# Layer 1's products of a two-layer decoder: one 512-column product and one of 256 columns against three of 256 columns, with one accumulator and displaced weight parts

## The chip, the cores and the metric

The kernel runs on one core of a Trainium2 chip. The metric is the device time of one execution in microseconds (us); less is better. Engines are named as in the profile: PE is the matrix engine, PEld its weight loads, DVE the vector engine, ACT the scalar engine, POOL GpSimd, SP the engine that issues the weight transfers.

## The reference, cut to what matters

The model has 16 meta tokens and 256 tokens of input, 2048 features, two layers and a feed-forward width of 8192. Layer 0 uses forgetting attention; layer 1 uses stick-breaking attention on a shared K/V stream. The last step drops the meta tokens, so in layer 1 only the shared K/V needs all 272 tokens; queries, output projection and feed-forward need 256.

```
for layer in range(DEPTH):                      # DEPTH = 2
    a = rms_norm(h, norm_attn[layer])
    if layer < N_A_LAYERS:
        proj = a @ fox_w_in[i]                  # q, k, v, forget gate
        h = h + forgetting_attention(...) @ fox_w_o[i]
    else:
        k_s, v_s = jnp.split(rms_norm(h, kv_norm) @ w_kv, 2, axis=-1)
        h = h + stick_breaking_attention(a @ sb_w_q[i], k_s, v_s) @ sb_w_o[i]
    h = h + jnp.square(jax.nn.relu(rms_norm(h, norm_mlp[layer]) @ w_up[layer])) @ w_down[layer]
return rms_norm(h, final_norm)[:, N_META:]
```

All of it is in float32, and the answer has to be near float32.

## The kernel before, in words

**Parts.** Activations are kept transposed: 16 chunks of 128 features, tokens along the row. A float32 number is multiplied on PE in the format float32r, which keeps fewer bits, so each operand is written as a sum of two parts, `hi` (rounded) and `lo` (the rest). A product of weight and activation is then three products: hi·hi, hi·lo and lo·hi; lo·lo is dropped. `Split` (L118) holds both parts of the 16 activation chunks in one tile with rows of 640 floats (`XROW`, L28); `ROWS` (L27) gives where in the row hi and lo begin: floats 48 and 368 in layer 0's tiles (272 tokens), 0 and 304 in layer 1's (256 tokens). The K/V stream of layer 1 has 272 tokens and layer 0's form.

**A group.** `gemm_group` (L183) computes 512 output features: four accumulators of 128 x 512 floats in PSUM (`accs`, L191), one for each m = 0..3. The 16 chunks of the contraction come in four steps kb of four chunks kc. Each step loads two transfers of 512 KB from SP (L207); ACT rounds the weights to `whi` (L218), DVE writes `wlo` as the difference (L219). The tiles `whi` and `wlo` have rows of 576 floats. `whi` is written from float 0 of the row; `wlo` from float 0 in layer 0's groups and from float 16 (64 bytes) in layer 1's groups that run in pairs (L211). In the build the tiles of weights and activations all begin at multiples of 256 bytes, and so do their rows.

**Order.** In kb 0 and 3 a run is one m with four kc, in kb 1 and 2 two kc with four m (L226 to L231). The products are chained so that PE gets them as written (`gemm_matmul`, L175; the profile gives all of them line L177). Each product has its own weight load.

- Layer 0's products (and K/V of layer 1) come one by one with 272 columns: for each m and kc `whi`·hi, `whi`·lo, `wlo`·hi into the same columns of the accumulator (L244 to L250).
- Layer 1's groups (query projection, output projection, up and down, 40 groups) run in pairs: in each run first all `whi` products, each with 512 columns, which read hi and lo of the chunk in one go (`sp.both`, L130) and write them into the two halves of the accumulator; then all `wlo`·hi products with 256 columns into the first half (L236 to L243).
- One m of the last group, the argument `apart` (L493), is done product by product as in layer 0.

**After a group.** Each accumulator is drained by `evac`. With two halves the residual add (L255) has two DVE instructions, and the query and up projections call `total` (L259), where ACT copies the second half (L263) and DVE adds the first (L264) ahead of the work that follows.

Of the kernel before, what the change touches and what calls it, by code (L numbers as in the profile page):

```python
# [12 lines left out]
ALU = mybir.AluOpType  # L13
AX = mybir.AxisListType

P = 128
# [7 lines left out]
QSCALE = 1.0 / math.sqrt(P)  # L24
N_FF = 4

ROWS = {0: (48, 368), M: (0, 304)}  # L27
XROW = 640  # L28

G_A0, G_M0, G_KV, G_A1, G_M1, G_FIN = range(6)  # L30
# [3 lines left out]
def yoco_kernel(ctx: ExitStack, tc: tile.TileContext, hT_in, gains, b_f, w_f, w_qkv0, w_o0, w_up, w_dn,  # L34
# [83 lines left out]
    class Split:  # L118


        def __init__(self, label, t0):
            n = T - t0
            self.t0 = t0
            rows = xs.tile([P, NC * XROW + 64], F32R, tag="x", name=f"x_{label}")
            hi, lo = ROWS[t0]
            rows = rows[:, hi:hi + NC * XROW].rearrange("p (c t) -> p c t", c=NC)
            d = lo - hi
            self.hi, self.lo = rows[:, :, :n], rows[:, :, d:d + n]

            self.both = rows[:, :, :2 * d].rearrange("p c (i t) -> p c i t", i=2)[:, :, :, :n]  # L130

    def split_chunk(sp, gi, c):

        g = g_sb[:, gi, c:c + 1]
# [45 lines left out]
                                                                        mybir.DependencyReason.DATA))  # L180
        queued[:] = [ins]

    def gemm_group(wblk, sp, t0, evac, before={}, after={}, load_x=None, pairs=False, apart=()):  # L183

        uid[0] += 1
        u = uid[0]  # L190
        accs = [pacc.tile([P, 512], F32, tag="acc", name=f"acc_{u}_{m}") for m in range(4)]  # L191
        n = T - t0
        for kb in range(4):
            src_w = wblk[kb].rearrange("p (k c) -> p k c", k=4)
            if kb in before:
                before[kb]()
            piece = 1 if load_x is not None and kb < 2 else 2
            raws = [wraw.tile([P, 2, 512], F32, tag="raw", name=f"raw_{u}_{kb}_{hf}") for hf in range(2)]
            for k0 in range(0, 4, piece):
                if load_x is not None:  # L200
                    load_x(range(4 * kb + k0, 4 * kb + k0 + piece))
                if load_x is not None and kb == k0 == 0:

                    for c0 in (0, 256):
                        nc.scalar.dma_start(raws[0][:, 0, c0:c0 + 256], src_w[:, 0, c0:c0 + 256])
                else:
                    nc.sync.dma_start(raws[k0 // 2][:, k0 % 2:k0 % 2 + piece], src_w[:, k0:k0 + piece])  # L207
            parts = []
            for hf in range(2):
                whi, wlo = (wspl.tile([P, 2, 576], F32R, tag=f"w{x}", name=f"w{x}_{u}_{kb}_{hf}") for x in ("hi", "lo"))  # L210
                whi, wlo = whi[:, :, :512], wlo[:, :, 16:528] if pairs else wlo[:, :, :512]  # L211
                boxes = [(o, piece, 0, 512) for o in range(0, 2, piece)]
                if load_x is not None and kb == hf == 0:
                    boxes[:1] = [(0, 1, 0, 256), (0, 1, 256, 512)]
                for o, no, c0, c1 in boxes:
                    src = raws[hf][:, o:o + no, c0:c1]
                    hp, lp = whi[:, o:o + no, c0:c1], wlo[:, o:o + no, c0:c1]
                    on_act = nc.scalar.activation(hp, src, AF.Copy)  # L218
                    on_dve = nc.vector.tensor_tensor(out=lp, in0=src, in1=hp.bitcast(F32), op=ALU.subtract)  # L219
                parts.append((whi, wlo))  # L220
            if kb in after:
                with tc.issue_after(on_act.ins), tc.issue_after(on_dve.ins):
                    after[kb]()


            if load_x is not None and kb == 0:  # L226
                runs = [([kc], range(4)) for kc in range(4)]
            elif kb in (0, 3):
                runs = [(range(4), [m]) for m in range(4)]
            else:  # L230
                runs = [(range(2 * hf, 2 * hf + 2), range(4)) for hf in range(2)]  # L231
            pinned[0] = load_x is None
            for kcs, ms in runs:
                paired = [m for m in ms if pairs and m not in apart]
                single = [m for m in ms if m not in paired]
                for kc in kcs:  # L236
                    for m in paired:
                        gemm_matmul(accs[m], parts[kc // 2][0][:, kc % 2, m * P:(m + 1) * P], sp.both[:, 4 * kb + kc],
                                    start=kb == kc == 0, stop=False)
                for kc in kcs:  # L240
                    for m in paired:
                        gemm_matmul(accs[m][:, :n], parts[kc // 2][1][:, kc % 2, m * P:(m + 1) * P],
                                    sp.hi[:, 4 * kb + kc], start=False, stop=kb == kc == 3)  # L243
                for m in single:  # L244
                    for kc in kcs:
                        wh, wl = (w[:, kc % 2, m * P:(m + 1) * P] for w in parts[kc // 2])
                        hi, lo = sp.hi[:, 4 * kb + kc], sp.lo[:, 4 * kb + kc]
                        gemm_matmul(accs[m][:, :n], wh, hi, start=kb == kc == 0, stop=False)
                        gemm_matmul(accs[m][:, :n], wh, lo, start=False, stop=False)
                        gemm_matmul(accs[m][:, :n], wl, hi, start=False, stop=kb == kc == 3)  # L250
                if kb == 3:
                    for m in ms:
                        evac(m, [accs[m][:, :n]] + ([accs[m][:, n:]] if m in paired else []))

    def residual_add(c, acc, t0):  # L255
        for a in acc:
            nc.vector.tensor_tensor(out=hT[:, c, t0:], in0=a, in1=hT[:, c, t0:], op=ALU.add)  # L257

    def total(acc, to):  # L259

        if len(acc) == 1:
            return acc[0]
        nc.scalar.copy(to, acc[1])  # L263
        nc.vector.tensor_tensor(out=to, in0=acc[0], in1=to, op=ALU.add)  # L264
        return to


    norm = Norm("a0", 0)
# [96 lines left out]
    for g in range(4):  # L365
# [2 lines left out]
        vT = att.tile([P, 4, T], F32, tag="vT", bufs=1, name=f"vT0_{g}")  # L368

        def evac_q(m, acc, qT=qT):  # L370
            nc.vector.scalar_tensor_tensor(out=qT[:, m, :], in0=acc[0], scalar=-QSCALE, in1=box["rstd"],
                                           op0=ALU.mult, op1=ALU.mult)

        def evac_kv(m, acc, t):
            nc.vector.tensor_tensor(out=t[:, m, :], in0=acc[0], in1=box["rstd"], op=ALU.mult)

        if g == 0:

            gemm_group(w_qkv0[0], xa, 0, lambda m, acc, qT=qT: nc.scalar.copy(qT[:, m, :], acc[0]),
                       after={kb: (lambda kb=kb: first_norm(kb)) for kb in range(4)}, load_x=load_x)  # L380
            gate_products()
            box["rstd"] = norm.finish()
            for m in range(4):
                evac_q(m, [qT[:, m, :]])
            forget_gates(box["rstd"])
        else:
            gemm_group(w_qkv0[3 * g], xa, 0, evac_q)
# [88 lines left out]
    def out_proj(w, ao, t0, gi, label):  # L476
        norm = Norm(label, t0)
        xm = Split(label, t0)
        for g in range(4):
            def evac(m, acc, g=g):  # L480
                c = 4 * g + m
                residual_add(c, acc, t0)
                split_chunk(xm, gi, c)
                norm.add(c)
            gemm_group(w[g], ao, t0, evac, pairs=t0 == M)
        return xm, norm

    def mlp(layer, xm, norm, t0, last_evac):
# [5 lines left out]
        for f in range(N_FF):  # L494
            u = Split(f"u{layer}_{f}", t0)
            for g in range(4):
                def evac(m, acc, g=g):
                    c = 4 * g + m
                    r = tmp.tile([P, T], F32, tag="relu", name=f"relu_{layer}_{f}_{c}")
                    u2 = tmp.tile([P, T], F32, tag="u2", name=f"u2_{layer}_{f}_{c}")  # L500
                    nc.vector.scalar_tensor_tensor(out=r[:, t0:], in0=total(acc, r[:, t0:]), scalar=0.0, in1=box["r"][:, t0:],
                                                   op0=ALU.max, op1=ALU.mult)
                    nc.scalar.activation(u2[:, t0:], r[:, t0:], AF.Square)
                    nc.scalar.activation(u.hi[:, c], u2[:, t0:], AF.Copy)
                    nc.vector.tensor_tensor(out=u.lo[:, c], in0=u2[:, t0:], in1=u.hi[:, c].bitcast(F32),
                                            op=ALU.subtract)
                gemm_group(w_up[layer, f, g], xm, t0, evac, {2: get_rstd} if f == g == 0 else {},
                           pairs=t0 == M)
            for g in range(4):
                def evac(m, acc, g=g):  # L510
                    residual_add(4 * g + m, acc, t0)
                    if f == N_FF - 1:
                        last_evac(4 * g + m)
                gemm_group(w_dn[layer, f, g], u, t0, evac, pairs=t0 == M,
                           apart=(3,) if layer == 1 and f == N_FF - 1 and g == 3 else ())

    xm, norm_m = out_proj(w_o0, ao, 0, G_M0, "m0")

# [17 lines left out]
    for g in range(4):  # L536
        def evac_q1(m, acc, g=g):
            q = qT1[g][:, m, :S]
            nc.vector.scalar_tensor_tensor(out=q, in0=total(acc, q), scalar=QSCALE, in1=box["rstd"][:, M:],
                                           op0=ALU.mult, op1=ALU.mult)  # L540
        def split_c(kb, g=g):
            for c in ([4 * kb + g - 1] if g < 3 else [4 * kb + 2, 4 * kb + 3]):
                split_chunk(xc, G_KV, c)

        gemm_group(w_q1[g], xq, M, evac_q1, {2: get_rstd1} if g == 0 else {},
                   after={kb: (lambda kb=kb: split_c(kb)) for kb in range(4)} if g else {}, pairs=True)

    ao = Split("o1", M)
    for g in range(4):
# [189 lines left out]
```

## Time and profile before

| | |
|---|---|
| median of 3 runs | 2315.99 us (2315.36 to 2316.57) |
| profiled execution | 2316.17 us, its span 2314.5 us |
| PE busy | 2303.4 us (100%), 16486 products |
| PEld busy | 2183.1 us (94%), 16486 loads |
| DVE, ACT, POOL busy | 1350.1 us (58%), 1064.1 us (46%), 40.8 us (2%) |
| granted PE clock, mean | 0.998 |
| DMA | 412 MB, 178 GB/s |

How to read it: a product of float32 (not float32r) stands in two records, so records are more than products in the program; a few records may be missing. A product is pipelined: its record lasts longer than the time until the next one starts, so what a product costs is the distance between starts. In a timeline, neighbouring instructions of one kind are merged: start, length from the first start to the last end, kind, and count. The first product of layer 1's query projection starts at about 1200 us, its K/V and attention lie between about 1304 and 1521 us; the output projection begins among the last of that work and lasts until about 1597 us, up and down from there to 2302 us.

### The profile page before, as it was taken

What the parts mean: (1) busy time and instruction counts of PE and PEld (TensorE: products, weight loads), DVE (VectorE), ACT (ScalarE), POOL (GpSimd) and SP (SyncE); (2) the same over time, 40 slices, a digit from 0 to 9 for tenths busy, and PEclk for the clock granted to TensorE, in tenths of its full rate; (3) what the DMA queues carried; (4) which work ended last, traced back from release to release, by engine and by line L of the source; (5) the groups of instructions that cost most, each with busy time, mean ns of one, the idle gap of its engine ahead of it and who ended that gap; (6) DMA issues with size and microseconds to landing.
All of it is one profiled execution on the core that took longest, in us unless ns stands there. A gap on an engine that the chain in (4) does not pass through costs nothing.

```text
span 2314.5 us, 39954 instructions
## 1 busy us (share of the span) xinstructions
PE 2303.4 (100%) x16486; PEld 2183.1 (94%) x16486; DVE 1350.1 (58%) x1923; ACT 1064.1 (46%) x1477; POOL 40.8 (2%) x58
## 2 busy tenths in 40 slices
PE   9999999999999999999999999999999999999998
PEld 9999999999999999999998999988888888888887
DVE  7665555655454455445566555566665665665665
ACT  6434344543344344344445444455543543543553
POOL 1000000000000000000000000000000000000000
PEclk9999999999999999999999999999999999999999
DMA  6545445455555555555555444455556556556563
GB/s 233 169 155 170 166 163 170 168 187 174 181 170 186 179 175 181 173 184 175 182 178 200 157 146 146 146 169 196 193 188 199 185 190 200 185 191 199 183 200 128
DMA packets 116630, 412.00 MB, mean 178 GB/s; under 512 B 13264, under 2 KB 16736, under 8 KB 116448
## 3 DMA queue, kind: packets, MB, share of 16 engines
q1 hardware_dynamic: 114560, 406.29, 52.7%
q10 hardware_dynamic: 1888, 3.16, 0.4%
q8 instruction: 129, 2.11, 0.4%
q14 instruction: 53, 0.43, 0.1%
HBM read 407.29 MB, written 2.11 MB: 177 GB/s over the span
## 4 chain that ended last, share of the span: by engine, by line
PE 99%; DVE 0%; DMA 0%; ACT 0%; issue 0%; SPq 0%; DVEq 0%; ACTq 0%
PE acc L177 96%; PE ps L407 0%; PE pza L586 0%; PE pv L340 0%; PE po L469 0%; PE po L625 0%; PE pzb L587 0%; PE po L626 0%; PE po L470 0%; DMA g_sb<-gains 0%; PE po L627 0%; DVE ob L681 0%; PE pf L306 0%; PE pf L307 0%; PE pta L601 0%; PE pta L602 0%
## 5 line engine op out<-in xcount | busy, mean ns | idle before, releaser
L219 DVE TENSOR_TENSOR wlo<-raw,whi 128x1024 fp32r<-128x1024 f32 (+1 forms) x773 | 931.6, 1217 | 741.8 <-ACT whi L218 740.6
L218 ACT ACTIVATE whi<-raw 128x1024 fp32r<-128x1024 f32 (+1 forms) x773 | 799.1, 1050 | 948.0 <-PE acc L177 873.8
L177 PE MATMUL acc<-x_u,whi 128*128 128x272 f32 (+2 forms) x3088 | 647.9, 321 | 0.0
L177 PE MATMUL acc<-x_m,whi 128*128 128x272 f32 (+1 forms) x3072 | 646.2, 322 | 0.0
L177 PEld LDWEIGHTS acc<-x_u,whi 128*128 128x128 f32 x3088 | 499.5, 188 | 26.6
L177 PEld LDWEIGHTS acc<-x_m,whi 128*128 128x128 f32 x3072 | 497.5, 188 | 27.2
L177 PE MATMUL acc<-x_u,wlo 128*128 128x272 f32 (+1 forms) x2048 | 443.3, 281 | 0.0
L177 PE MATMUL acc<-x_m,wlo 128*128 128x272 f32 (+1 forms) x2048 | 441.0, 281 | 0.0
L177 PE MATMUL acc<-x_a,whi 128*128 128x272 f32 (+1 forms) x1792 | 360.6, 306 | 0.1
L177 PEld LDWEIGHTS acc<-x_u,wlo 128*128 128x128 f32 x2048 | 338.4, 188 | 15.8
L177 PEld LDWEIGHTS acc<-x_m,wlo 128*128 128x128 f32 x2048 | 337.5, 188 | 15.9
L177 PEld LDWEIGHTS acc<-x_a,whi 128*128 128x128 f32 x1792 | 284.2, 188 | 9.4 <-issue 0.7
L177 PE MATMUL acc<-x_a,wlo 128*128 128x272 f32 (+1 forms) x1024 | 254.0, 286 | 0.0
L177 PE MATMUL acc<-x_kv,whi 128*128 128x272 f32 x1024 | 194.1, 288 | 0.0
L177 PEld LDWEIGHTS acc<-x_a,wlo 128*128 128x128 f32 x1024 | 179.1, 188 | 5.3 <-DVE wlo L219 0.6
L177 PE MATMUL acc<-x_o,whi 128*128 128x272 f32 (+1 forms) x768 | 162.4, 322 | 0.0
L177 PEld LDWEIGHTS acc<-x_kv,whi 128*128 128x128 f32 x1024 | 160.6, 188 | 0.4
L177 PE MATMUL acc<-x_kv,wlo 128*128 128x272 f32 x512 | 147.3, 288 | 0.0
L257 DVE TENSOR_TENSOR hT<-acc,hT 128x256 f32<-128x256 f32 (+1 forms) x239 | 102.4, 428 | 70.5 <-PE acc L177 68.8
L177 PEld LDWEIGHTS acc<-x_o,whi 128*128 128x128 f32 x768 | 124.3, 188 | 6.7
L177 PE MATMUL acc<-x_o,wlo 128*128 128x272 f32 (+1 forms) x512 | 111.0, 282 | 0.0
L177 PEld LDWEIGHTS acc<-x_kv,wlo 128*128 128x128 f32 x512 | 96.5, 188 | 0.1
(226 smaller groups left out, 1040.0 us busy)
## 6 DMA issues: line engine op xcount, KB each, us to landing
raw<-w_up SPq DMA_DIRECT2D x256, 512.0 KB, 4.7
raw<-w_dn SPq DMA_DIRECT2D x256, 512.0 KB, 4.8
raw<-w_qkv SPq DMA_DIRECT2D x92, 512.0 KB, 4.3
raw<-w_o SPq DMA_DIRECT2D x64, 512.0 KB, 4.4
raw<-w_kv SPq DMA_DIRECT2D x64, 512.0 KB, 3.9
raw<-w_q SPq DMA_DIRECT2D x32, 512.0 KB, 4.8
fk<-f_dram ACTq DMA_DIRECT2D x4, 544.0 KB, 5.1
raw<-w_qkv SPq DMA_DIRECT2D x7, 256.0 KB, 4.6
```

The costliest lines, as they stand in the source:

```text
L177: ins = nc.tensor.matmul(*args, **kw).ins
L218: on_act = nc.scalar.activation(hp, src, AF.Copy)
L219: on_dve = nc.vector.tensor_tensor(out=lp, in0=src, in1=hp.bitcast(F32), op=ALU.subtract)
L257: nc.vector.tensor_tensor(out=hT[:, c, t0:], in0=a, in1=hT[:, c, t0:], op=ALU.add)
```

## The change

All products of layer 1's groups become 256 columns wide: in each run first all `whi`·hi, then all `whi`·lo, then all `wlo`·hi, all into the same 256 columns of one accumulator. `whi` and `wlo` are both written from float 16 (64 bytes) of their rows in groups that have 256 tokens, and lo begins at float 320 of the activation's row in place of 304. `sp.both`, `pairs`, `apart` and `total` go. Layer 0's products and those of K/V keep order, width and places.

```
-ROWS = {0: (48, 368), M: (0, 304)}
+ROWS = {0: (48, 368), M: (0, 320)}
...
-                whi, wlo = whi[:, :, :512], wlo[:, :, 16:528] if pairs else wlo[:, :, :512]
+                o = 16 if t0 else 0
+                whi, wlo = whi[:, :, o:o + 512], wlo[:, :, o:o + 512]
...
-                paired = [m for m in ms if pairs and m not in apart]
-                single = [m for m in ms if m not in paired]
-                for kc in kcs:
-                    for m in paired:
-                        gemm_matmul(accs[m], parts[kc // 2][0][:, kc % 2, m * P:(m + 1) * P], sp.both[:, 4 * kb + kc],
-                                    start=kb == kc == 0, stop=False)
-                for kc in kcs:
-                    for m in paired:
-                        gemm_matmul(accs[m][:, :n], parts[kc // 2][1][:, kc % 2, m * P:(m + 1) * P],
-                                    sp.hi[:, 4 * kb + kc], start=False, stop=kb == kc == 3)
-                for m in single:
-                    for kc in kcs:
-                        wh, wl = (w[:, kc % 2, m * P:(m + 1) * P] for w in parts[kc // 2])
-                        hi, lo = sp.hi[:, 4 * kb + kc], sp.lo[:, 4 * kb + kc]
-                        gemm_matmul(accs[m][:, :n], wh, hi, start=kb == kc == 0, stop=False)
-                        gemm_matmul(accs[m][:, :n], wh, lo, start=False, stop=False)
-                        gemm_matmul(accs[m][:, :n], wl, hi, start=False, stop=kb == kc == 3)
+                pairs = ((0, sp.hi), (0, sp.lo), (1, sp.hi))
+                if t0:
+                    products = [(kc, m, *pair) for pair in pairs for kc in kcs for m in ms]
+                else:
+                    products = [(kc, m, *pair) for m in ms for kc in kcs for pair in pairs]
+                left = {m: 3 * len(kcs) for m in ms}
+                for kc, m, part, x in products:
+                    first, left[m] = kb == kc == 0 and left[m] == 3 * len(kcs), left[m] - 1
+                    gemm_matmul(accs[m][:, :n], parts[kc // 2][part][:, kc % 2, m * P:(m + 1) * P], x[:, 4 * kb + kc],
+                                start=first, stop=kb == kc == 3 and left[m] == 0)
                 if kb == 3:
                     for m in ms:
-                        evac(m, [accs[m][:, :n]] + ([accs[m][:, n:]] if m in paired else []))
+                        evac(m, accs[m][:, :n])
 
     def residual_add(c, acc, t0):
-        for a in acc:
-            nc.vector.tensor_tensor(out=hT[:, c, t0:], in0=a, in1=hT[:, c, t0:], op=ALU.add)
-
-    def total(acc, to):
-
-        if len(acc) == 1:
-            return acc[0]
-        nc.scalar.copy(to, acc[1])
-        nc.vector.tensor_tensor(out=to, in0=acc[0], in1=to, op=ALU.add)
-        return to
+        nc.vector.tensor_tensor(out=hT[:, c, t0:], in0=acc, in1=hT[:, c, t0:], op=ALU.add)
```

In the built program the instructions up to the end of layer 0 stand in the same order on each engine. Behind it PE has 2544 instructions more, ACT 80 fewer and DVE 159 fewer; SP and POOL have the same in the same order.

More of the change, by code (lines that the diff above doesn't have):

```diff
@@ L128, in __init__ @@
             self.hi, self.lo = rows[:, :, :n], rows[:, :, d:d + n]
-            self.both = rows[:, :, :2 * d].rearrange("p c (i t) -> p c i t", i=2)[:, :, :, :n]
     def split_chunk(sp, gi, c):
@@ L181, in gemm_matmul, with gemm_group @@
         queued[:] = [ins]
-    def gemm_group(wblk, sp, t0, evac, before={}, after={}, load_x=None, pairs=False, apart=()):
+    def gemm_group(wblk, sp, t0, evac, before={}, after={}, load_x=None):
         uid[0] += 1
@@ L370, in evac_q @@
         def evac_q(m, acc, qT=qT):
-            nc.vector.scalar_tensor_tensor(out=qT[:, m, :], in0=acc[0], scalar=-QSCALE, in1=box["rstd"],
+            nc.vector.scalar_tensor_tensor(out=qT[:, m, :], in0=acc, scalar=-QSCALE, in1=box["rstd"],
                                            op0=ALU.mult, op1=ALU.mult)
         def evac_kv(m, acc, t):
-            nc.vector.tensor_tensor(out=t[:, m, :], in0=acc[0], in1=box["rstd"], op=ALU.mult)
+            nc.vector.tensor_tensor(out=t[:, m, :], in0=acc, in1=box["rstd"], op=ALU.mult)
         if g == 0:
-            gemm_group(w_qkv0[0], xa, 0, lambda m, acc, qT=qT: nc.scalar.copy(qT[:, m, :], acc[0]),
+            gemm_group(w_qkv0[0], xa, 0, lambda m, acc, qT=qT: nc.scalar.copy(qT[:, m, :], acc),
                        after={kb: (lambda kb=kb: first_norm(kb)) for kb in range(4)}, load_x=load_x)
@@ L383, in yoco_kernel @@
             for m in range(4):
-                evac_q(m, [qT[:, m, :]])
+                evac_q(m, qT[:, m, :])
             forget_gates(box["rstd"])
@@ L484, in evac @@
                 norm.add(c)
-            gemm_group(w[g], ao, t0, evac, pairs=t0 == M)
+            gemm_group(w[g], ao, t0, evac)
         return xm, norm
@@ L500, in evac @@
                     u2 = tmp.tile([P, T], F32, tag="u2", name=f"u2_{layer}_{f}_{c}")
-                    nc.vector.scalar_tensor_tensor(out=r[:, t0:], in0=total(acc, r[:, t0:]), scalar=0.0, in1=box["r"][:, t0:],
+                    nc.vector.scalar_tensor_tensor(out=r[:, t0:], in0=acc, scalar=0.0, in1=box["r"][:, t0:],
                                                    op0=ALU.max, op1=ALU.mult)
@@ L506, in evac @@
                                             op=ALU.subtract)
-                gemm_group(w_up[layer, f, g], xm, t0, evac, {2: get_rstd} if f == g == 0 else {},
-                           pairs=t0 == M)
+                gemm_group(w_up[layer, f, g], xm, t0, evac, {2: get_rstd} if f == g == 0 else {})
             for g in range(4):
@@ L513, in evac @@
                         last_evac(4 * g + m)
-                gemm_group(w_dn[layer, f, g], u, t0, evac, pairs=t0 == M,
-                           apart=(3,) if layer == 1 and f == N_FF - 1 and g == 3 else ())
+                gemm_group(w_dn[layer, f, g], u, t0, evac)
     xm, norm_m = out_proj(w_o0, ao, 0, G_M0, "m0")
@@ L538, in evac_q1 @@
             q = qT1[g][:, m, :S]
-            nc.vector.scalar_tensor_tensor(out=q, in0=total(acc, q), scalar=QSCALE, in1=box["rstd"][:, M:],
+            nc.vector.scalar_tensor_tensor(out=q, in0=acc, scalar=QSCALE, in1=box["rstd"][:, M:],
                                            op0=ALU.mult, op1=ALU.mult)
@@ L545, in yoco_kernel @@
         gemm_group(w_q1[g], xq, M, evac_q1, {2: get_rstd1} if g == 0 else {},
-                   after={kb: (lambda kb=kb: split_c(kb)) for kb in range(4)} if g else {}, pairs=True)
+                   after={kb: (lambda kb=kb: split_c(kb)) for kb in range(4)} if g else {})
     ao = Split("o1", M)
```

## The prediction

> **What bounds the kernel now.** I read the page first: span, busy time by engine, the granted clock, and the chain that ended last.
>
> ```profile
> span 2314.5 us, 39954 instructions
> ...
> PE 2303.4 (100%) x16486; PEld 2183.1 (94%) x16486; DVE 1350.1 (58%) x1923; ACT 1064.1 (46%) x1477; POOL 40.8 (2%) x58
> ...
> PEclk9999999999999999999999999999999999999999
> ...
> PE 99%; DVE 0%; DMA 0%; ACT 0%; issue 0%; SPq 0%; DVEq 0%; ACTq 0%
> ```
>
> PE is busy in 2303.4 of 2314.5 us, its clock is never withheld, and the chain that sets the end is 99% PE. So the kernel lasts as long as the starts of its products lie apart, and the question is what three 256-column products cost beside one of 512 and one of 256. How many are changed is in the groups by shape, over the whole span:
>
> ```profile
> L177 PE MATMUL acc<-x_m,whi 128*128 128x512 f32 x1024 | 266.9, 392 | 0.0
> L177 PE MATMUL acc<-x_u,whi 128*128 128x512 f32 x1008 | 262.9, 392 | 0.0
> ...
> L177 PE MATMUL acc<-x_o,whi 128*128 128x512 f32 x256 | 67.2, 393 | 0.0
> L177 PE MATMUL acc<-x_a,whi 128*128 128x512 f32 x256 | 66.9, 393 | 0.0
> ```
>
> 1024 + 1008 + 256 + 256 = 2544 products of 512 columns, which is 40 groups of 64 less the 16 of the last group's separate m. Before none of them did PE sit idle (last column 0.0). Their mean record, 392 ns, is a latency; the cost is in the starts. This is the timeline of PE alone, in a down projection of layer 1; each row begins when its first product begins, so a row's cost is the next row's start less its own:
>
> ```profile
> 1707.39 1.08 PE L177 MATMUL acc<-x_u,whi 128*128 128x512 f32 x4
> 1708.31 0.62 PE L177 MATMUL acc<-x_u,wlo 128*128 128x256 f32 x4
> 1708.77 1.08 PE L177 MATMUL acc<-x_u,whi 128*128 128x512 f32 x4
> 1709.69 0.62 PE L177 MATMUL acc<-x_u,wlo 128*128 128x256 f32 x4
> 1710.14 1.08 PE L177 MATMUL acc<-x_u,whi 128*128 128x512 f32 x4
> 1711.06 0.62 PE L177 MATMUL acc<-x_u,wlo 128*128 128x256 f32 x4
> 1711.51 1.08 PE L177 MATMUL acc<-x_u,whi 128*128 128x512 f32 x4
> 1712.43 0.62 PE L177 MATMUL acc<-x_u,wlo 128*128 128x256 f32 x4
> 1712.89 2.00 PE L177 MATMUL acc<-x_u,whi 128*128 128x512 f32 x8
> 1714.73 1.07 PE L177 MATMUL acc<-x_u,wlo 128*128 128x256 f32 x8
> 1715.63 2.00 PE L177 MATMUL acc<-x_u,whi 128*128 128x512 f32 x8
> 1717.47 1.07 PE L177 MATMUL acc<-x_u,wlo 128*128 128x256 f32 x8
> 1718.38 2.00 PE L177 MATMUL acc<-x_u,whi 128*128 128x512 f32 x8
> 1720.22 1.07 PE L177 MATMUL acc<-x_u,wlo 128*128 128x256 f32 x8
> 1721.13 2.00 PE L177 MATMUL acc<-x_u,whi 128*128 128x512 f32 x8
> 1722.97 1.07 PE L177 MATMUL acc<-x_u,wlo 128*128 128x256 f32 x8
> 1723.87 1.08 PE L177 MATMUL acc<-x_u,whi 128*128 128x512 f32 x4
> ```
>
> From 1707.39 to 1723.87 stand 48 pairs in 16.48 us: **343.3 ns a pair**. The eight wlo stretches take 0.46 + 0.45 + 0.45 + 0.46 + 0.90 + 0.91 + 0.91 + 0.90 = 5.44 us, **113.3 ns** a 256-column product; the rest, 11.04 us, makes **230.0 ns** a 512-column product. So 512 columns cost 3.4 ns more than twice 256: the wide product is no bargain here.
>
> Two more rows give 256 and 272 columns under other conditions. The first two rows are the separate m of the last group, 12 products from one to the other; the next two are layer 0, in which 15 repeats of three products lie between the first row and the last:
>
> ```profile
> 2282.82 0.41 PE L177 MATMUL acc<-x_u,whi 128*128 128x256 f32 x2
> ...
> 2284.24 1.54 PE L177 MATMUL acc<-x_u,whi 128*128 128x512 f32 x6
> ```
>
> ```profile
> 135.07 0.28 PE L177 MATMUL acc<-x_a,wlo 128*128 128x272 f32 x1
> ...
> 140.62 0.29 PE L177 MATMUL acc<-x_a,wlo 128*128 128x272 f32 x1
> ```
>
> The separate m costs 1.42 us / 12 = 118.3 ns a product of 256 columns, 5 ns more than in a wlo stretch; layer 0 costs 5.55 us / 45 = 123.3 ns a product of 272.
>
> **The change part by part.**
>
> *Products.* 2544 pairs of 343.3 ns become triples. `wlo`·hi stays as it is. What are `whi`·hi and `whi`·lo worth? The wlo stretches are the nearest row, for these reasons. A wlo stretch has weights that begin 64 bytes past a multiple of 256 and activations that begin on one. After the change all three kinds have this: `whi` moves to float 16 (64 bytes), lo from float 304 (1216 bytes, 192 past a multiple of 256) to 320 (1280 bytes, on one). The stretches with one m and four kc and those with four m and two kc cost the same, so neither a new row of activations nor the same accumulator again costs anything. And the 118.3 ns come from exactly what goes: `whi` at 0, lo at 304. In layer 0 weights also lie 64 bytes past the activations, modulo 256, for hi and lo alike (weights at 0, hi and lo at 192). From both sides: at best a 256-column product costs what PE needed where it moves 128-column float32 data, which the timeline has for transposes:
>
> ```profile
> 177.43 0.60 PE L340 MATMUL pv<-ident,vT 128*128 128x128 f32 x4
> ```
>
> Four records, the last one 0.27 us long (the same row, if the three distances are 109 ns), so 109 ns each with a 128-column load every time. At worst it costs the 118.3 of the separate m. I take 113.3: three make 339.9 ns, 3.4 less than the pair. 2544 x 3.4 ns = **-8.6 us**. The ends are 2544 x (327 - 343.3) = -41.5 us and 2544 x (354.9 - 343.3) = +29.5 us.
>
> *The separate m.* 16 chunks of three products go from 118.3 to 113.3 ns: 48 x 5 ns = **-0.2 us**.
>
> *Weight loads.* 2544 more, each beside the product ahead of it. In a wlo stretch a load goes with each 113.3 ns without PE sitting idle, so I charge nothing; were the load the slower one, it would show as a longer distance and is inside the bounds above.
>
> *Draining.* ACT loses 80 copies and DVE 80 adds of `total` and 79 second residual adds. Of the up projection:
>
> ```profile
> L264 DVE TENSOR_TENSOR relu<-acc,relu 128x256 f32<-128x256 f32 x64 | 27.1, 424 | 16.1 <-ACT relu L263 16.1
> L263 ACT COPY relu<-acc 128x256 f32<-128x256 f32 x64 | 23.7, 370 | 39.3 <-PE acc L177 39.3
> ```
>
> That frees some 30 us of ACT (80 x 370 ns) and 67 us of DVE (159 x 424 ns), all beside PE, which had not waited for them: **0**. The accumulators come free 0.4 to 0.8 us earlier, and nothing is late at that point. DVE and ACT still cut the weights in the same order, one group of 64 triples needing 21.75 us in place of 21.97; SP's transfers keep their order and come 1% closer. At the end of the kernel the last m was a separate one before, so the chain behind it is the same: 0.
>
> *Where layer 1's attention ends*, a few of its products move by one or two places among the first of the output projection. PE stays fed there; I allow 0.5 us either way.
>
> The sum: -8.6 - 0.2 = -8.8 us against the profiled execution's 2316.17 us, which is 0.18 us over the median of the three runs: **2307.3 us**, -0.38%. What the measurement tells from no change is about 0.2%, 4.6 us.
>
> **The rivals.**
>
> *A fixed cost for each product (slower).* Layer 0's 123.3 ns at 272 columns and 230.0 ns at 512 lie on a line: 106.7 ns for 240 columns, 0.4446 ns a column, and 2.4 ns that don't depend on width. On it 256 columns cost 116.2 ns, and a triple 348.6, 5.3 more than the pair: 2544 x 5.3 = +13.5 us, **2329.7 us**. Its place is each `whi` product that is halved; it decides from 115.0 ns for the two `whi` products on (2 x 115.0 + 113.3 = 343.3). For it: it joins the two most numerous shapes, and layer 0 has the same distance of 64 bytes. Against it: the 48 wlo products in the timeline lie 2.9 ns below the line at 256 columns, at a distance that all three kinds are to have. It holds if the quick pace belongs to something else in a wlo stretch, such as following 512-column products. *The Trainium skill, "TensorE: Matmul & The Clock Gate", section "Wait — 56ns, not 53.3ns?", has a rule on this side: back-to-back matmuls start columns / 2.4 GHz plus about 2.5 ns apart. By it the pair would cost 215.8 + 109.2 = 325.0 ns and the triple 327.5, so the change would add 2.5 ns x 2544, an estimate of +6.4 us, 2322.5 us. The trace has a constant as large on the line, but its 230.0 against 2 x 113.3 says that here the halves are the cheaper.*
>
> *Only hi runs quickly (no change).* The rows at 113.3 ns all move hi; lo could cost 116.2 ns with a load beside it. Then the triple is 342.8 ns, 0.5 less: -1.3 - 0.2, **2314.7 us**. Against it: in layer 0 the products of lo cost what those of hi cost, the repeats being even.
>
> *The displacement doesn't do what it is there for (slower).* If the 118.3 ns of the separate m come from going between `whi` and `wlo` or hi and lo at 256 columns, not from their places, all triples cost 354.9 ns: +29.5 us, **2345.7 us**. Against it: in the new order this happens once in four or eight products, in the separate m at each.
>
> *Quicker than any row of this width*, 109 ns: 2274.7 us. Nothing of float32r stands for it.
>
> **How the numbers follow.** 113.3 for all: 0.68. The fixed cost: 0.15. Only hi: 0.08. The separate m's pace: 0.06. 109 ns: 0.03. Faster by over 0.2% are the first and the last, 0.71; within it is "only hi", 0.08; slower are the other two, 0.21. The likeliest and "only hi" together hold 0.76, so the range has to reach to the fixed cost: from 2304 (the likeliest less 3 us, for a start distance 0.4 ns shorter) to 2331 us, which holds 0.91. The likeliest one's own range is 2304 to 2311.
>
> **What would show it.** In the timeline of layer 1, rows of 16 `whi` products that take 1.81 us from start to start and of 8 `wlo` products that take 0.90 or 0.91; 1.86 for the 16 would be the fixed cost, 1.89 the separate m's pace, and 1.84 lo alone. Layer 0 should keep its 123.3 ns, and the first product of the query projection its place at 1200 us. PEld should be near 100% busy in layer 1, the rows of L263 and L264 be gone, and PE's idle time remain 0.0. The forecast is wrong if the 256-column `whi` rows are over 115.0 ns, or if PE begins to wait for weights or for an accumulator.

## The result and the profile after

The changed kernel takes 2337.38 us (median of 5 runs, 2336.67 to 2337.68) against 2315.99 us: **1.0091 of the time before, 95% interval 1.0077 to 1.0106**. It is 21.4 us slower; the forecast was 8.8 us faster, and 2337.4 lies above the range that ended at 2331.

The page of the changed kernel, in the lines that answer to those shown of before:

```profile
span 2335.9 us, 44808 instructions
...
PE 2325.1 (100%) x19030; PEld 2312.5 (99%) x19030; DVE 1291.4 (55%) x1764; ACT 1041.1 (45%) x1397; POOL 39.7 (2%) x58
...
PE 99%; DMA 1%; DVE 0%; ACT 0%; issue 0%; SPq 0%; DVEq 0%; ACTq 0%
```

There is no new wait: PE is busy all the time, DVE and ACT do less than before, PEld has gone from 94% to 99%. The chain's 1% of DMA lies in the first 16 us of the kernel and costs nothing here: the query projection's first product starts at 1188.0 us against 1188.4 before. (That is its start in both traces, and not the 1200 us named ahead; K/V follows from 1277 us.) The products themselves must be slower. The groups of PE by shape have layer 1's 256-column `whi` products by the activations that they read:

```profile
L175 PE MATMUL acc<-x_u,whi 128*128 128x256 f32 x2048 | 272.8, 281 | 0.0
L175 PE MATMUL acc<-x_m,whi 128*128 128x256 f32 x2048 | 272.4, 281 | 0.0
...
L175 PE MATMUL acc<-x_a,whi 128*128 128x256 f32 x512 | 68.1, 281 | 0.0
L175 PE MATMUL acc<-x_o,whi 128*128 128x256 f32 x512 | 67.1, 277 | 0.0
```

The mean record gives the first hint: 281 ns in the feed-forward (x_u, x_m) and the query projection (x_a), 277 ns in the output projection (x_o). It is the same instruction with operands in the same places modulo 256 bytes. The starts say it plainly. This is the changed kernel's timeline of PE in the output projection:

```profile
1570.90 1.07 PE L175 MATMUL acc<-x_o,whi 128*128 128x256 f32 x8
1571.81 0.62 PE L175 MATMUL acc<-x_o,wlo 128*128 128x256 f32 x4
...
1581.78 1.41 PE L175 MATMUL acc<-x_o,whi 128*128 128x256 f32 x11
```

and this in the feed-forward:

```profile
1716.83 2.05 PE L175 MATMUL acc<-x_u,whi 128*128 128x256 f32 x16
1718.71 1.11 PE L175 MATMUL acc<-x_u,wlo 128*128 128x256 f32 x8
...
1725.31 0.87 PE L175 MATMUL acc<-x_u,whi 128*128 128x256 f32 x6
```

In the first, eight repeats of 8 + 4 products take 10.88 us, **113.3 ns** a product, as forecast. In the second, three repeats of 16 + 8 take 8.48 us, **117.8 ns**. One stage has the pace of the forecast, for `whi`·hi, `whi`·lo and `wlo`·hi alike; the other has a slower one, also for all three. And the slower one begins at a point. Here is the start of the feed-forward, around its norm product (`pms_m`, a float32 product of the sum of squares, ahead of step 2 of the first group):

```profile
1608.08 1.07 PE L175 MATMUL acc<-x_m,wlo 128*128 128x256 f32 x8
1608.99 0.59 PE L156 MATMUL pms_m<-ssq_m,mean_w 128*128 128x256 f32 x2
1609.23 2.23 PE L175 MATMUL acc<-x_m,whi 128*128 128x256 f32 x16
1611.30 1.10 PE L175 MATMUL acc<-x_m,wlo 128*128 128x256 f32 x8
1612.24 2.05 PE L175 MATMUL acc<-x_m,whi 128*128 128x256 f32 x16
```

Ahead of the norm product 8 products take 0.91 us (1608.08 to 1608.99), behind it 0.94 (1611.30 to 1612.24), and 0.94 or 0.95 it stays until the final norm's products, in the last 20 us of the kernel. The query projection has the same turn at its own norm product, at 1199 us. 672 products of the query projection and 6048 of the feed-forward come behind these two points: 6720 x 4.45 ns = 29.9 us. Without them the kernel would take 2307.5 us, and e9 below takes that.

The kernel before has the same norm product at the same point, but its `wlo` products keep their pace behind it, 0.91 us for 8 (1610.35 to 1611.26):

```profile
1608.08 0.59 PE L158 MATMUL pms_m<-ssq_m,mean_w 128*128 128x256 f32 x2
1608.33 2.19 PE L177 MATMUL acc<-x_m,whi 128*128 128x512 f32 x8
1610.35 1.07 PE L177 MATMUL acc<-x_m,wlo 128*128 128x256 f32 x8
1611.26 2.00 PE L177 MATMUL acc<-x_m,whi 128*128 128x512 f32 x8
```

### The profile page after: what moved, and what is told of

Its sections match the earlier page's. It is cut to its first block, busy times and chain, and to the rows that moved or that the text cites. A ratio compares the mean times of both kernels' runs of the same rounds, so it can differ in the third digit from the quotient of the medians.

```text
span 2335.9 us, 44808 instructions
## 1 busy us (share of the span) xinstructions
PE 2325.1 (100%) x19030; PEld 2312.5 (99%) x19030; DVE 1291.4 (55%) x1764; ACT 1041.1 (45%) x1397; POOL 39.7 (2%) x58
## 4 chain that ended last, share of the span: by engine, by line
PE 99%; DMA 1%; DVE 0%; ACT 0%; issue 0%; SPq 0%; DVEq 0%; ACTq 0%
PE acc L175 95%; DMA hT<-hT_in 1%; PE ps L387 0%; PE pza L564 0%; PE pv L320 0%; PE po L449 0%; PE po L603 0%; PE po L604 0%; PE pzb L565 0%; PE po L450 0%; PE po L605 0%; DVE ob L659 0%; PE pf L287 0%; PE pf L286 0%; PE pta L579 0%; PE pta L580 0%
## 5 line engine op out<-in xcount | busy, mean ns | idle before, releaser
L175 PE MATMUL acc<-x_u,whi 128*128 128x272 f32 (+1 forms) x4096 | 651.9, 284 | 0.0
L175 PEld LDWEIGHTS acc<-x_m,whi 128*128 128x128 f32 x4096 | 573.7, 189 | 0.1
L175 PEld LDWEIGHTS acc<-x_u,whi 128*128 128x128 f32 x4096 | 573.8, 189 | 0.0
L175 PEld LDWEIGHTS acc<-x_u,wlo 128*128 128x128 f32 x2048 | 327.6, 189 | 0.0
L175 PEld LDWEIGHTS acc<-x_m,wlo 128*128 128x128 f32 x2048 | 327.5, 189 | 0.0
L175 PEld LDWEIGHTS acc<-x_a,whi 128*128 128x128 f32 x2048 | 303.7, 189 | 2.1 <-issue 0.7
L175 PEld LDWEIGHTS acc<-x_o,whi 128*128 128x128 f32 x1024 | 141.9, 188 | 0.1
L245 DVE TENSOR_TENSOR hT<-acc,hT 128x272 f32<-128x272 f32 (+1 forms) x160 | 69.1, 432 | 88.1 <-PE acc L175 86.8
```

The costliest lines, as they stand in the source:

```text
L175: ins = nc.tensor.matmul(*args, **kw).ins
L245: nc.vector.tensor_tensor(out=hT[:, c, t0:], in0=acc, in1=hT[:, c, t0:], op=ALU.add)
```

## The experiments

**Theory A**: a stream of these products has two steady paces, 113.3 and 117.8 ns; the norm product throws it into the slow one, where it stays, and in the kernel before the 512-column products brought it back in each run. **Theory B**: the slow pace belongs to what runs beside the stage. **Theory C**: the distance between the places of weights and activations decides which paces there are. D and E came later. Each run is named by its label; where no interval is given, it is one execution.

**e1_wide_after_norm**: an unused 512-column product behind each norm product.

```
...
             pinned[0] = load_x is None
+            if t0 and kb in before:
+                wide = patt.tile([P, 512], F32, tag="patt", name=f"wide_{u}")
+                gemm_matmul(wide, parts[0][0][:, 0, :P], sp.both[:, 4 * kb], start=True, stop=True)
```

> The changed kernel plus one unused 512-column float32r product (whi against hi and lo of one chunk) straight behind each of layer 1's two norm products, which are float32; two products in all, about 0.23 us each. Theory A (the stream of 256-column products has two steady paces, 113.3 and 117.8 ns; a float32 product between them starts the slow one, and it lasts until something else breaks the stream; a 512-column product lets it start the quick one): 672 products of the query projection and 6048 of the feed-forward go from 117.8 to 113.3 ns, -29.9 us, +0.5 for the two products: 2308. Theory B (the slow pace belongs to what runs beside these stages, drains and splits and transfers, and not to how the stream was started): 2337.4 + 0.5 = 2338, with 117.8 ns in both stages.

Measured: 2307.95 us, 0.9966 of the kernel before (0.9953 to 0.9979). Its timeline of PE at the same place:

```profile
1605.92 0.59 PE L157 MATMUL pms_m<-ssq_m,mean_w 128*128 128x256 f32 x2
1606.16 0.59 PE L176 MATMUL wide<-x_m,whi 128*128 128x512 f32 x1
1606.59 1.99 PE L176 MATMUL acc<-x_m,whi 128*128 128x256 f32 x16
1608.42 1.07 PE L176 MATMUL acc<-x_m,wlo 128*128 128x256 f32 x8
1609.32 1.98 PE L176 MATMUL acc<-x_m,whi 128*128 128x256 f32 x16
1611.14 1.07 PE L176 MATMUL acc<-x_m,wlo 128*128 128x256 f32 x8
```

8 products now take 0.90 us behind the norm product and 16 take 1.82, and so it stays. Two products that compute nothing save 29.4 us. Theory B falls: drains, splits and transfers are the same.

**e6_narrow_after_norm**: the same extra product with 256 columns; the edit to e1's kernel:

```
-                gemm_matmul(wide, parts[0][0][:, 0, :P], sp.both[:, 4 * kb], start=True, stop=True)
+                gemm_matmul(wide[:, :n], parts[0][0][:, 0, :P], sp.hi[:, 4 * kb], start=True, stop=True)
```

> As the run with a 512-column product behind each norm product, but that product has 256 columns (whi against hi). If it is the width that lets the loads catch up (theory A), this one is only one more product of the stream: 117.8 ns stays, 2337.4 + 0.2 = 2338. If any float32r product that isn't accumulated or any shift of the starts would do: 113.3 ns, 2308.

Measured: 2337.81 us. In its timeline the stream behind the extra product takes 0.94 us for 8:

```profile
1609.27 0.47 PE L176 MATMUL wide<-x_m,whi 128*128 128x256 f32 x1
1609.58 2.05 PE L176 MATMUL acc<-x_m,whi 128*128 128x256 f32 x16
1611.46 1.11 PE L176 MATMUL acc<-x_m,wlo 128*128 128x256 f32 x8
1612.40 2.05 PE L176 MATMUL acc<-x_m,whi 128*128 128x256 f32 x16
```

So it is not one more product that helps here, but one that is wide (it also reads lo beside hi). Whether its width counts as such, or only how the stream starts again behind it, these two runs don't tell.

**e2_norm_float32r**: the norm's sum of squares cut into hi and lo, and two float32r products in place of the float32 one.

```
...
+                nc.scalar.activation(ahi[:, :n], self.acc[:, self.t0:], AF.Copy)
+                nc.vector.tensor_tensor(out=alo[:, :n], in0=self.acc[:, self.t0:], in1=ahi[:, :n].bitcast(F32),
+                                        op=ALU.subtract)
+                nc.tensor.matmul(ps[:, :n], mean_r, ahi[:, :n], start=True, stop=False)
+                nc.tensor.matmul(ps[:, :n], mean_r, alo[:, :n], start=False, stop=True)
...
```

> The changed kernel with layer 1's two norm products made of two float32r products (hi and lo part of the sum of squares) in place of one float32 product, so that no float32 product stands inside a stage of 256-column products. Theory A: nothing starts the slow pace, 113.3 ns in both stages, 2307 (up to 1 us more if PE waits for the two parts). Theory B: 117.8 ns stays, 2337.

Measured: 2310.11 us, 0.9974 (0.9964 to 0.9984). The feed-forward is quick (0.91 us for 8 behind its norm products), but not the query projection. There the norm products have 272 columns in place of 256, and their operands lie at other places too. Its timeline there:

```profile
1198.97 0.29 PE L165 MATMUL pms_a<-alo_a,mean_r 128*128 128x272 f32 x1
1199.10 2.05 PE L186 MATMUL acc<-x_a,whi 128*128 128x256 f32 x16
1200.98 1.10 PE L186 MATMUL acc<-x_a,wlo 128*128 128x256 f32 x8
1201.92 2.05 PE L186 MATMUL acc<-x_a,whi 128*128 128x256 f32 x16
```

0.94 us for 8: slow, behind a float32r product. 672 products x 4.45 ns = 3.0 us is about the difference to the 2307.5 us of e9. So the part of theory A that named float32 as the cause is wrong; a float32r product in the stream can start the slow pace too.

**e4_float32_in_outproj**: a float32 product of the same width where the stream was quick.

```
-            gemm_group(w[g], ao, t0, evac)
+            def stop_stream():
+                ps = patt.tile([P, 512], F32, tag="patt", name="ps_stop")
+                nc.tensor.matmul(ps[:, :S], mean_w, maskB[:, :S], start=True, stop=True)
+            gemm_group(w[g], ao, t0, evac, {2: stop_stream} if t0 and g == 1 else {})
```

> The changed kernel plus one unused float32 product of 256 columns (about 0.43 us) ahead of step 2 of the output projection's second group, where the stream runs at 113.3 ns. Theory A: from there to the end of the output projection, 480 products, 117.8 ns: +2.1 + 0.4 = 2340, and the timeline shows 16 whi products in 1.88 us there. Theory B: 113.3 ns on both sides of it, 2337.8.

Measured: 2338.11 us; theory A's number is missed. Theory B's is met, but e1 has ruled B out. The timeline behind the product:

```profile
1543.61 0.59 PE L467 MATMUL ps_stop<-maskB,mean_w 128*128 128x256 f32 x2
1543.85 2.20 PE L175 MATMUL acc<-x_o,whi 128*128 128x256 f32 x16
1545.89 1.07 PE L175 MATMUL acc<-x_o,wlo 128*128 128x256 f32 x8
1546.80 1.98 PE L175 MATMUL acc<-x_o,whi 128*128 128x256 f32 x16
```

The first run of 16 is held up as behind the norm product (2.04 us to the next row, there 2.07), but then the stream is quick, 0.91 us for 8. So a float32 product does not have to throw it. This one read an operand that lies 160 bytes past a multiple of 256 in the build. The tile of the sum of squares begins on one: the query projection's norm product reads it from there, the feed-forward's from 64 bytes behind, since it leaves out the 16 meta tokens. That made theory D: the interruption sets how the stream starts again, and the place of its data is enough to shift that. Its rival, theory E: the stage decides, and the feed-forward stays slow behind any float32 product.

**e5_sum_at_160**: the sum of squares that layer 1's two norm products read is moved to 160 bytes past a multiple of 256, by 160 bytes in the query projection and by 96 in the feed-forward (the expectation below takes 0 as the old place of both). The tile grows by 256 bytes, so what lies behind it keeps its place modulo 256.

```
-            self.acc = tmp.tile([P, T], F32, tag="ssq", bufs=1, name=f"ssq_{label}")
+            acc = tmp.tile([P, T + 64], F32, tag="ssq", bufs=1, name=f"ssq_{label}")
+            o = 40 - t0 if label in ("a1", "m1") else 0
+            self.acc = acc[:, o:o + T]
```

> The changed kernel; only the place of the sum of squares that layer 1's two norm products read is changed, from 0 to 160 bytes past a multiple of 256, which is where the operand of the float32 product of the run with one in the output projection lay (after that one the stream found back to 113.3 ns). Theory D (which pace the stream takes up is decided by how its first products and loads fall after the interruption, and the place of the interrupting product's data shifts that): the feed-forward runs at 113.3 ns, 2308 if the query projection does too, 2311 if not. Theory E (it is decided by the stage: activations and weights of the feed-forward stay in the slow pace after any float32 product): 117.8, 2337.

Measured: 2307.53 us. The timeline at the norm product:

```profile
1606.03 0.59 PE L158 MATMUL pms_m<-ssq_m,mean_w 128*128 128x256 f32 x2
1606.27 2.20 PE L177 MATMUL acc<-x_m,whi 128*128 128x256 f32 x16
1608.31 1.07 PE L177 MATMUL acc<-x_m,wlo 128*128 128x256 f32 x8
1609.22 1.98 PE L177 MATMUL acc<-x_m,whi 128*128 128x256 f32 x16
```

The same float32 product, as long as before (0.59 us), at the same place of the order, with the same weights and activations around it: 0.91 us for 8 behind it. Theory E falls, D stands.

**e9_best_sum_at_160**: the same kernel, timed in five rounds.

> The kernel of the run with the sum of squares at 160 bytes again, now timed: the changed kernel without the slow pace. Theory A and D: 2307.5 in each execution, 0.9963 of the kernel before. If the pace that the stream takes up differed from execution to execution, some would be near 2311 (query projection slow), 2334 (feed-forward slow) or 2337.

Measured: 2307.51 us (2307.17 to 2307.78), **0.9962 of the kernel before (0.9949 to 0.9976)**. It beats both kernels. The five times lie within 0.6 us, so the pace was the quick one in each; a stage in the slow pace would have added 3 us or more.

**e3_no_displacement, e7_displacement_128, e8_displacement_192**: the changed kernel with both weight parts at 0, 128 and 192 bytes. The edit of e7; e3 has 0 and e8 has 48 in place of 32:

```
-                o = 16 if t0 else 0
+                o = 32 if t0 else 0
```

> The changed kernel with both weight parts at float 0 of their rows in layer 1 too (no displacement; lo still at float 320). Theory A alone says nothing of places: 113.3 ns in the output projection and 117.8 in the feed-forward as before, 2337. Theory C (the quick pace exists only with the 64 bytes, as the separate m of the kernel before, at 118.3 ns, suggested): 118 ns or more in the output projection too, 768 x 4.7 = 3.6 us more, 2341 or over.

> The changed kernel with both weight parts displaced by 128 bytes in place of 64. With 0 bytes all products took 120.0 ns, with 64 there are two paces, 113.3 and 117.8. If the distance sets which paces exist (theory C, as the run with no displacement bore it out): a third set of paces, at 120.0 in all stages or between 113.3 and 120; no float32 product changes it where there is only one. If only the presence of a displacement counts: the times of 64 bytes, 2337.

> The changed kernel with both weight parts displaced by 192 bytes. Theory C: a set of paces of its own, one pace or two, each between 113.3 and 120.0 ns, so 2307 to 2358. If only the presence of a displacement counts: 2337.

Measured: 2357.68, 2357.60 and 2341.07 us. In the timelines 24 products take, with 0 bytes, 2.88 us both in the output projection and here in the feed-forward (1800.40 to 1803.28):

```profile
1800.40 2.08 PE L175 MATMUL acc<-x_m,whi 128*128 128x256 f32 x16
...
1803.28 2.08 PE L175 MATMUL acc<-x_m,whi 128*128 128x256 f32 x16
```

With 128 bytes, 2.84 us in the output projection and 2.88 in the feed-forward:

```profile
1569.91 2.06 PE L175 MATMUL acc<-x_o,whi 128*128 128x256 f32 x16
...
1572.75 2.06 PE L175 MATMUL acc<-x_o,whi 128*128 128x256 f32 x16
...
1800.22 2.09 PE L175 MATMUL acc<-x_m,whi 128*128 128x256 f32 x16
...
1803.10 2.09 PE L175 MATMUL acc<-x_m,whi 128*128 128x256 f32 x16
```

With 192 bytes, 2.83 us in both; in the feed-forward:

```profile
1813.98 2.05 PE L175 MATMUL acc<-x_m,whi 128*128 128x256 f32 x16
...
1816.81 2.04 PE L175 MATMUL acc<-x_m,whi 128*128 128x256 f32 x16
```

Over the long stretches of the traces that is 120.0 ns at 0 bytes, 118.7 and 120.0 at 128, 117.8 at 192, and 113.3 or 117.8 at 64. So the place of the weights decides which paces were seen, as theory C said, and theory D is about which of them the stream takes up. Of the four places only 64 bytes showed the quick pace, and it is also one of the two that showed two. These runs moved the weights alone; whether their distance from the activations counts, or their own place, they don't tell.

**e10_512_displaced**: the kernel before with the change's places and without its split.

```
-ROWS = {0: (48, 368), M: (0, 304)}
+ROWS = {0: (48, 368), M: (0, 320)}
...
-                whi, wlo = whi[:, :, :512], wlo[:, :, 16:528] if pairs else wlo[:, :, :512]
+                o = 16 if pairs else 0
+                whi, wlo = whi[:, :, o:o + 512], wlo[:, :, o:o + 512]
```

> The kernel before with the places alone changed: whi too at 64 bytes and lo at float 320, the products still 512 and 256 columns wide. If the 3.4 ns by which a 512-column product was dearer than two of 256 came from the places (whi at 0, lo 192 past a multiple of 256), it now takes 226.7 ns and the time is 2316.2 - 8.6 = 2307.6; the width keeps the stream quick behind the norm products. If the 3.4 ns belong to the width: 230.0 ns, 2316.

Measured: 2323.77 us, slower than before, which neither reading expected. The timeline:

```profile
1710.95 1.09 PE L177 MATMUL acc<-x_u,whi 128*128 128x512 f32 x4
1711.88 0.62 PE L177 MATMUL acc<-x_u,wlo 128*128 128x256 f32 x4
...
1715.11 2.02 PE L177 MATMUL acc<-x_u,whi 128*128 128x512 f32 x8
```

12 pairs take 4.16 us, 346.7 ns a pair in place of 343.3. The new places cost the 512-column products time; alone they lose 7.4 us in this one execution. For the 256-column ones e3 shows that they are needed. Split and places belong together.

**e11_layer0_order, e12_layer0_place**: e5 with layer 0's products in layer 1's order, and with layer 0's tiles in layer 1's places.

```
-                if t0:
+                if t0 or load_x is None:
                     products = [(kc, m, *pair) for pair in pairs for kc in kcs for m in ms]
```

```
-ROWS = {0: (48, 368), M: (0, 320)}
+ROWS = {0: (0, 320), M: (0, 320)}
...
-                o = 16 if t0 else 0
+                o = 16
```

> The run with the sum at 160 bytes, with layer 0's and K/V's 272-column products (but the first group) in layer 1's order: whi with hi, whi with lo, wlo with hi, in runs. If 123.3 ns is a slow pace of these products that comes from the changing order: 16 columns more than 113.3 ns at 0.44 ns each, 120.4 ns, some 10500 products, -30 us, 2277. If the order plays no part, as in the comparison of the runs of layer 1: 2307.5.

> The run with the sum at 160 bytes, with layer 0's tiles in layer 1's places: weights 64 bytes past a multiple of 256, hi and lo on one (floats 0 and 320); the distance between them is what it was. If only the distance counts: 123.3 ns as before, 2307.5. If activations that begin on a multiple of 256 matter by themselves: another pace in layer 0, between 120.4 ns (2277) and 125 (2325).

Measured: 2307.06 and 2308.26 us, within 0.05% of e5. Layer 0's products cost 123.3 ns in both. So the order plays no part in them, and moving weights and activations together changes nothing. That fits the distance as what counts, but it is no proof: whether another distance changes these 272-column products at all was not tried.

One thing did change in e12, where layer 1's products have the places that they have in e5. The first 96 products of the query projection, which follow layer 0's without any other product between them, run slowly, 0.94 us for 8; behind the norm product they run quickly, 0.91:

```profile
1187.66 1.10 PE L177 MATMUL acc<-x_a,whi 128*128 128x256 f32 x8
1188.60 0.63 PE L177 MATMUL acc<-x_a,wlo 128*128 128x256 f32 x4
...
1198.97 0.62 PE L158 MATMUL pms_a<-ssq_a,mean_w 128*128 128x272 f32 x2
...
1201.25 1.07 PE L177 MATMUL acc<-x_a,wlo 128*128 128x256 f32 x8
1202.16 1.98 PE L177 MATMUL acc<-x_a,whi 128*128 128x256 f32 x16
```

In e5 both stretches are quick. So the slow pace can begin without an odd product in the stream, and a norm product, with its operand at 160 bytes, can end it: here an interruption chose the pace anew, in either direction.

## Why the prediction was wrong, point by point

- *What bounds the kernel*: right. The whole difference lies in the distance between the starts of products; PE's idle time stayed at 0.0 and no other engine entered.
- *The pair at 343.3 ns*: right, and 2544 products more, as counted.
- *Products, "I take 113.3"*: **the step that failed.** 113.3 ns is what all three kinds cost in most of the output projection, and in e5 in the query projection and the feed-forward too, and e5's time is 2307.5 us against the forecast 2307.3. What failed is the reading that a pace measured in short stretches belongs to the operands' places. The wlo stretches of before were four or eight products long, and each followed 512-column products. e1 and e6 show that one such product is enough to set the stream to the quick pace (e5 shows that it isn't the only way). With the wide products the restarts went too, and that left the stream in the pace that it took up behind the norm product: 6720 products x 4.45 ns = +29.9 us against the -8.8 us that did arrive.
- *The rival of the fixed cost* named the right condition, that the quick pace "belongs to something else in a wlo stretch, such as following 512-column products", but joined it to a wrong mechanism and price: 116.2 ns for halved products everywhere. The runs show 113.3 or 117.8 for all three kinds, by stage. That is why the range ended at 2331.
- *Only hi runs quickly*: wrong; lo cost what hi cost in each stage.
- *The displacement doesn't do what it is there for*: wrong as put, since without it the products cost 120.0 ns (e3); its price of 118.3 ns lies near the measured slow pace of 117.8, and whether that has the same reason is open.
- *Loads, drains, attention's end*: right at nothing; DVE and ACT went down and no wait came up.

What stays open is why the place of the norm's operand decides, and what holds the slow pace. That loads and products disturb each other in reading would fit the effect of the places, but is not shown.

## What to carry to other kernels

A distance between starts that was measured in short stretches holds for a long stream only if nothing in between had restarted it: look at what stands ahead of each stretch before carrying its pace to another order. Where a stage that PE bounds has products of one shape, compare its pace from stage to stage and at each odd product in it; a change of a few ns that begins at one instruction and stays can be a second pace, as it was here, where moving that instruction's operand or one wide product behind it ended it. Try the place of the weights in steps of 64 bytes for each product width by itself, since here the best place of one width was a worse one for another.

## What the runs showed of the hardware that was not expected

- A stream of 256-column float32r products, each with its own load, kept 113.3 ns (e5) or 117.8 ns (the changed kernel) over some 6000 products in a row in the feed-forward. The five executions of either timed kernel (the changed one and e9) lie within 1.1 us.
- With the activations on a multiple of 256 bytes, the pace hung on how far behind one the weights began: 120.0 ns at 0, 113.3 or 117.8 at 64, 118.7 or 120.0 at 128, 117.8 at 192. The Trainium skill, "TensorE: Matmul & The Clock Gate", section "Step-by-step: what each phase is for", says that loading the next weights doesn't take read bandwidth from the running matmul. The runs neither bear that out nor refute it: moving the weights alone from 64 to 0 bytes cost 2.2 or 6.7 ns a product, but whether through the load itself or through its effect on the running product isn't shown.
- Behind the norm product, one 512-column product of 0.43 us brought the stream back to the quick pace (e1), a 256-column one did not (e6). Moving the norm product's operand did it too (e5).
